# A hybrid decoder layer on one core: the orders of the engines planned by the scheduler's timeline simulation instead of its plain timing

## The chip, the cores and the metric

One core of a Trainium2 chip. TensorE (PE) multiplies matrices, VectorE (DVE), ScalarE (ACT) and GpSimd (POOL) work elementwise, and SyncE (SP) mostly starts DMA transfers; ACT and POOL start some too. The metric is the device time of one execution in microseconds, the median of several runs.

## The reference

One layer on x of 1024 tokens by 1024 channels, all in float32. With rmsnorm(x, g) = x · rsqrt(mean(x²) + eps) · g:

```
h = x
f = swiglu(rmsnorm(h, ffn1_pre_g), ffn1_w_gu, ffn1_w_down)     # 1024 -> 2 x 2816 -> 1024
h = h + 0.5 * rmsnorm(f, ffn1_post_g)
m = hybrid_mixer(rmsnorm(h, mix_pre_g), w_in, ...)              # below
h = h + rmsnorm(m, mix_post_g)
c = memory_cross_attention(rmsnorm(h, xa_pre_g), rmsnorm(mem, mem_g), xa_wq, xa_wkv, xa_wo)
h = h + rmsnorm(c, xa_post_g)
f = swiglu(rmsnorm(h, ffn2_pre_g), ffn2_w_gu, ffn2_w_down)
h = h + 0.5 * rmsnorm(f, ffn2_post_g)
```

The mixer projects its input, runs 16 heads of stick-breaking attention (width 64, blocks of 128) on one half of the projection and a chunked state-space scan (SSD: 16 heads, 2 groups, state 128, chunks of 128, after a short convolution) on the other, normalises both, and multiplies the two by w_out. The cross-attention has 4 heads of 256 over 256 memory tokens.

## The kernel before, in words

Everything is kept transposed, channels on partitions, and the tokens are two halves of 512. Every product of matrices is made of three passes of a reduced-precision float type: an operand is split into a high part, which ScalarE casts (line 263, or line 270 with a scale), and a low part, the difference, which VectorE subtracts (line 265 or 272). TensorE multiplies high by high, low by high and high by low (line 138). So each weight tile and each activation passes through a cast and a subtraction before TensorE can use it. In the names, whi and wlo are the parts of a weight, xh and xl, S, hl, ohi and olo those of an activation; wraw and raw are weights as loaded, mm and dn banks of PSUM with sums, ms the bank of the norms.

The stages follow one another in the profiled execution like this: ffn1 up to about 450 us, ffn1 down to 690, SSD to 1016, attention to 1585, mix_out (the product with w_out) to 1740, cross-attention to 1985, ffn2 up to 2440, ffn2 down to the end. In the ffn stages, after a few plain tiles, sums and differences of operands are formed so that seven products do for eight (a Strassen step): GpSimd adds weights (line 737), ScalarE scales blocks of the input that are loaded again (line 666), VectorE combines them (lines 676 and 679), ScalarE and VectorE split the result; the epilogue adds the seven results (lines 793 to 818).

A norm works like this: squares are made on ScalarE and added on VectorE (`sumsq`, lines 374 to 385), a column product on TensorE sums over channels (`rms_cols`, line 317; in the rows ms<-small,acc), a square root on ScalarE, which needs its table loaded, and a reciprocal on VectorE give the factors, and two row products with a diagonal matrix (`rms_rows`, line 341; ms<-dg and ms<-rpre or ms<-rn) spread them over partitions. Later steps multiply sums in PSUM by these rows and so let the banks free.

What sets the order: the author has fixed TensorE's. `_pe` (line 100) ties each matmul to the one before it by a dependence without a semaphore:

```
if self.prev is not None:
    self._after(ins, self.prev)
self.prev = ins
```

Only groups inside `with self.pinned(at)` (line 144), which are column and row products of norms, are not in this chain: each group has to come before the matmul at which a clock of the author's own passes `at`, and where before that is left to the scheduler. Work put on a list for later is emitted at fixed points of that clock and kept in program order (`kp`, line 117), and a few steps have a raised priority (`urgent`, line 96). All else, the orders on VectorE, ScalarE and GpSimd and that of the loads on SyncE, is chosen by the scheduler, which runs a model of the engines over the whole program and issues at each time what is ready, by priority. The allocation of slots in SBUF and PSUM pools follows from that order. The scheduler is set up in `build`, line 2412.

Of the kernel before, what the change touches and what calls it, by code (L numbers as in the profile page):

```python
# [2402 lines left out]
def build(arrays):  # L2403
    nc = bacc.Bacc("TRN2", target_bir_lowering=False, num_devices=1)
    ap = {
        n: nc.dram_tensor(f"in_{n}", v.shape, mybir.dt.from_np(v.dtype), kind="ExternalInput").ap()
        for n, v in arrays.items()
    }
    ap["out"] = [
        nc.dram_tensor(n, v, F32, kind="ExternalOutput").ap() for n, v in (("out_a", (H, D_MODEL)), ("out_b", (H, D_MODEL)))  # L2410
    ]
    with tile.TileContext(nc) as tc:
        Kern(nc, tc, ap).run()
    return nc

# [7 lines left out]
```

## Time and profile before

| | |
|---|---|
| median of 3 runs | 2643.67 us (2641.38 to 2644.43) |
| profiled execution, and its span | 2645.18 us, 2643.4 us |
| busy: PE, DVE, ACT, POOL | 2576.9, 1983.2, 1262.9, 530.8 us |
| mean granted clock of TensorE | 0.992 |
| moved by DMA | 528.87 MB, 200 GB/s |

A row of the timeline has a start and a length in us, the engine, the line, the operation, out<-in by the program's names, and in brackets how long the engine stood idle before it and who released it. A row of the waits has who waited for whom, and the us in total, the times and the longest. Times count from the span's start. A matmul of 512 columns is 0.39 us long but overlaps the next; they start 0.227 us apart when nothing holds them.

### The profile page before, as it was taken

Reading aid. Unit: us, or ns where it says so; the run is one execution under the profiler, and the core shown is the slowest. Engines: PE = TensorE matmul, PEld = TensorE weight load, DVE = VectorE, ACT = ScalarE, POOL = GpSimd, SP = SyncE. Lnnn points to the kernel's source line nnn. Section 1 sums busy time; section 2 is a strip of 40 time slices with the busy share of each in tenths; the row PEclk is TensorE's granted clock in tenths of the full one; section 3 lists DMA queues with packets and bytes.
Section 4 is the critical chain, followed back from the end, with each engine's and each line's share of the span. In section 5 each row is a group of like instructions: output and inputs, shape, how many; then the busy total and the mean of one; then the engine's idle time right before and its main releaser. Section 6 shows DMA issues by size and latency. Waiting matters only on the chain.

```text
span 2643.4 us, 36454 instructions
## 1 busy us (share of the span) xinstructions
PE 2576.9 (97%) x12598; PEld 2135.0 (81%) x12598; DVE 1983.2 (75%) x3085; ACT 1262.9 (48%) x2276; POOL 530.8 (20%) x660
## 2 busy tenths in 40 slices
PE   8999999999999999999999998999999999999998
PEld 6788888887777778888888787887878788888887
DVE  7888787888678774777777777775448989895675
ACT  7544443545367783445554445254445433333432
POOL 1555552001100000000000001122012555542000
PEclk9999999999999999999999999999999999999999
DMA  5688887754721226433434458777667455555976
GB/s 209 238 308 302 304 282 252 255 193 158 259 79 45 71 70 196 115 99 108 109 108 115 146 178 323 252 274 252 218 230 272 167 187 203 195 180 210 347 276 218
DMA packets 225241, 528.87 MB, mean 200 GB/s; under 512 B 28064, under 2 KB 35104, under 8 KB 225056
## 3 DMA queue, kind: packets, MB, share of 16 engines
q1 hardware_dynamic: 190432, 419.56, 48.2%
q0 software_dynamic: 27424, 93.87, 9.8%
q10 hardware_dynamic: 7200, 13.11, 1.3%
q8 instruction: 99, 1.62, 0.3%
q14 instruction: 86, 0.70, 0.1%
HBM read 353.41 MB, written 152.04 MB: 191 GB/s over the span
## 4 chain that ended last, share of the span: by engine, by line
PE 79%; DVE 9%; DMA 6%; ACT 3%; issue 2%; POOL 1%; SPq 0%; DVEq 0%; ACTq 0%; POOLq 0%
PE mm L138 45%; PE dn L138 24%; PE z L138 2%; PE ms L138 2%; PE tr L141 2%; PE y L138 1%; PE ms L141 1%; DMA wraw<-act 1%; DMA raw<-act 1%; DVE hl L265 1%; DVE wlo L265 1%; PE seg L138 1%; DMA blk<-h 1%; DVE whi L265 0%; DMA oraw<-mix 0%
## 5 line engine op out<-in xcount | busy, mean ns | idle before, releaser
L138 PE MATMUL mm<-xh,whi 128*128 128x512 f32 x1288 | 511.5, 406 | 11.1 <-ACT xh L270 7.0
L138 PE MATMUL mm<-xh,wlo 128*128 128x512 f32 x1240 | 478.5, 393 | 3.2 <-DVE wlo L265 2.9
L138 PE MATMUL mm<-xl,whi 128*128 128x512 f32 x1188 | 467.8, 394 | 1.0 <-DVE xl L265 0.7
L138 PEld LDWEIGHTS mm<-xh,whi 128*128 128x128 f32 x1288 | 244.1, 189 | 53.6 <-ACT xh L270 6.9
L138 PEld LDWEIGHTS mm<-xh,wlo 128*128 128x128 f32 x1240 | 234.3, 189 | 55.3 <-DVE wlo L265 3.4
L138 PEld LDWEIGHTS mm<-xl,whi 128*128 128x128 f32 x1188 | 225.6, 190 | 34.1 <-DVE xl L265 1.8
L1823 DVE TENSOR_TENSOR_SCAN nb<-nb,begin 128x128 f32<-128x128 f32 (+7 forms) x128 | 171.7, 1352 | 55.0 <-ACT nb L1819 54.4
L1819 ACT ACTIVATE nb<-z,scale 128x128 f32<-128x128 f32 (+2 forms) x192 | 107.8, 580 | 88.8 <-PE z L138 87.7
L263 ACT CAST whi<-wraw 128x1024 fp32r<-128x1024 f32 (+1 forms) x89 | 81.2, 914 | 69.1 <-PE mm L138 39.1
L1856 POOL MEMSET ath<- 128x128 f32 x64 | 13.1, 205 | 499.0 <-PE mm L138 499.0
L265 DVE TENSOR_TENSOR wlo<-wraw,whi 128x1024 fp32r<-128x1024 f32 x61 | 74.4, 1220 | 38.3 <-ACT whi L263 38.0
L138 PE MATMUL dn<-xh,wlo 128*128 128x512 f32 x296 | 101.0, 389 | 0.0
L737 POOL TENSOR_TENSOR wc<-wraw,raw 128x512 f32<-128x512 f32 x57 | 87.5, 1535 | 66.6 <-DVE whi L265 30.7
L737 POOL TENSOR_TENSOR wc<-raw,wraw 128x512 f32<-128x512 f32 x55 | 85.5, 1555 | 66.5 <-DVE wlo L265 31.4
L819 POOL TENSOR_TENSOR ft<-ft,e 128x512 f32<-128x512 f32 x38 | 62.4, 1642 | 144.2 <-DVE e L818 85.7
L650 ACT ACTIVATE ft<-ft 128x512 f32<-128x512 f32 x88 | 55.4, 631 | 75.0 <-DVE ft L649 70.3
L263 ACT CAST ath<-tr 128x512 fp32r<-128x512 f32 (+1 forms) x107 | 58.2, 545 | 67.5 <-PE tr L141 66.1
L138 PE MATMUL dn<-xh,blk 128*128 128x512 f32 x280 | 90.2, 389 | 0.0
L265 DVE TENSOR_TENSOR atl<-tr,ath 128x512 fp32r<-128x512 f32 (+1 forms) x107 | 67.0, 629 | 29.2 <-ACT ath L263 28.9
L138 PE MATMUL dn<-xh,whi 128*128 128x512 f32 x256 | 88.0, 389 | 0.0
L138 PE MATMUL mm<-ath,v 128*128 128x256 f32 x320 | 86.2, 291 | 0.6 <-DVE sq L1838 0.6
L382 DVE TENSOR_TENSOR acc<-acc,sq 128x512 f32<-128x512 f32 x78 | 52.3, 684 | 42.5 <-ACT sq L381 42.2
(586 smaller groups left out, 6667.9 us busy)
## 6 DMA issues: line engine op xcount, KB each, us to landing
whi<-dwhi SPq DMA_DIRECT2D x57, 512.0 KB, 3.4
wlo<-dwlo SPq DMA_DIRECT2D x57, 512.0 KB, 4.2
wraw<-act SPq DMA_DIRECT2D x102, 256.0 KB, 4.4
raw<-act SPq DMA_DIRECT2D x96, 256.0 KB, 4.3
wraw<-in_w_gu SPq DMA_DIRECT2D x44, 512.0 KB, 4.4
raw<-in_w_gu SPq DMA_DIRECT2D x38, 512.0 KB, 4.8
khi<-whi POOLq DMA_DIRECT2D x30, 512.0 KB, 4.6
klo<-wlo POOLq DMA_DIRECT2D x30, 512.0 KB, 6.7
```

What stands on the lines that cost most here:

```text
L138: self._pe(self.nc.tensor.matmul(out, lhsT, rhs, start=start, stop=stop, skip_group_check=self.more), cost)
L141: self._pe(self.nc.tensor.transpose(out, src, self.ident if ident is None else ident), 109.0)
L263: self.kp(self.nc.scalar.copy(hi, src))
L265: (eng or self.nc.vector).tensor_tensor(out=lo, in0=src, in1=hi.bitcast(F32), op=ALU.subtract)
L382: self.kp(nc.vector.tensor_tensor(out=accs[i % 2], in0=accs[i % 2], in1=sq, op=ALU.add))
L650: nc.scalar.activation(t, t, AF.Silu)
L737: nc.gpsimd.tensor_tensor(out=t, in0=a, in1=b, op=op)
L819: nc.gpsimd.tensor_tensor(out=t1, in0=t1, in1=e, op=ALU.mult)
L1819: nc.scalar.activation(nb[:, s0:s1], z[:, 0:n], AF.Sigmoid, scale=sc[:, i : i + 1])
L1823: nc.vector.tensor_tensor_scan(out=nb[:, 0:Wd][:, ::-1], data0=nb[:, 0:Wd][:, ::-1], data1=begin[:, S - Wd : S][:, ::-1], initial=0.0, op0 ...
L1856: nc.gpsimd.memset(x[:, 0, :].bitcast(F32), 0.0)
```

## The change

The one changed line tells the scheduler to plan with its timeline simulation, another model of how long instructions take and when they are ready, where it used its plain timing. The program that goes into the scheduler, every operation and every tile, is the same; priorities, the fixed chain on TensorE and the program order of later work still hold.

```
-    with tile.TileContext(nc) as tc:
+    with tile.TileContext(nc, schedule_with_timeline_sim=True) as tc:
```

What comes out differs. On TensorE ten floating norm groups take other places (168 lines of difference on 9885 rows), and nothing else moves. On VectorE 2326 lines differ, on ScalarE 1314, on SyncE 950, on GpSimd 205. ScalarE has 59 table loads where it had 56. 360 tiles get another slot.

At the start of the program, on ScalarE, the splits of the first half of x (xh), the squares of the first norm (acc, sq) and the casts of the first weights (whi) stand like this before:

```order
L263 CAST whi_196<-wraw_194 128x1024
L270 ACTIVATE xh_4_80<-S_68_182,params_78 128x512
L270 ACTIVATE xh_5_81<-S_68_182,params_78 128x512
L270 ACTIVATE xh_6_82<-S_69_183,params_78 128x512
L270 ACTIVATE xh_7_83<-S_69_183,params_78 128x512
L270 ACTIVATE xh_8_84<-S_70_184,params_78 128x512
L270 ACTIVATE xh_9_85<-S_70_184,params_78 128x512
L270 ACTIVATE xh_10_86<-S_71_185,params_78 128x512
L270 ACTIVATE xh_11_87<-S_71_185,params_78 128x512
L378 ACTIVATE acc_87_236<-S_68_182 128x512
L378 ACTIVATE acc_88_237<-S_68_182 128x512
L263 CAST whi_226<-wraw_224 128x1024
```

Now, from the second of those squares to the same cast:

```order
L378 ACTIVATE acc_88_237<-S_68_182 128x512
L270 ACTIVATE xh_6_82<-S_69_183,params_78 128x512
L381 ACTIVATE sq_89_240<-S_69_183 128x512
L270 ACTIVATE xh_7_83<-S_69_183,params_78 128x512
L381 ACTIVATE sq_90_243<-S_69_183 128x512
L270 ACTIVATE xh_8_84<-S_70_184,params_78 128x512
L270 ACTIVATE xh_9_85<-S_70_184,params_78 128x512
L270 ACTIVATE xh_10_86<-S_71_185,params_78 128x512
L381 ACTIVATE sq_91_246<-S_70_184 128x512
L270 ACTIVATE xh_11_87<-S_71_185,params_78 128x512
L381 ACTIVATE sq_92_249<-S_70_184 128x512
L263 CAST whi_226<-wraw_224 128x1024
```

Of the eight squares of that norm, two stood ahead of the cast whi_226, and now six do, between the splits.

In the same stretch, on TensorE, the column products of that norm (ms_260) among the third weight tile's matmuls (mm_418), the second piece of the difference (in the first, the group's old place goes, behind xh_6):

```order
 L138 MATMUL mm_418<-xh_9_85,wlo_282 128x512
 L138 MATMUL mm_418<-xh_10_86,whi_281 128x512
+L138 MATMUL ms_260<-small_114,acc_87_236 128x1 x4
 L138 MATMUL mm_418<-xl_26_102,whi_281 128x512
 L138 MATMUL mm_418<-xh_10_86,wlo_282 128x512
 L138 MATMUL mm_418<-xh_11_87,whi_281 128x512
-L138 MATMUL ms_274<-dg_270,onesr_115 128x512
 L138 MATMUL mm_418<-xl_27_103,whi_281 128x512
 L138 MATMUL mm_418<-xh_11_87,wlo_282 128x512
+L138 MATMUL ms_274<-dg_270,onesr_115 128x512
 L138 MATMUL ms_274<-rpre_99_271,onesr_115 128x512
```

The group went from behind the seventh of the tile's matmuls to behind the nineteenth, twelve matmuls on; its row products (ms_274) went two on, to the end of the tile.

In the first seven-product of ffn1 up, on ScalarE, the scale of the last operand block (blk_945), the casts of operands (xh) and the casts of weight sums (whi, wlo; wc is a sum made by GpSimd) before:

```order
L666 ACTIVATE blk_861<-blk_861,params_78 128x512
L666 ACTIVATE blk_945<-blk_945,params_78 128x512
L263 CAST blk_1010<-wc_1008 128x512
L263 CAST xh_14_90<-bl_952 128x512
L263 CAST blk_1029<-wc_1027 128x512
L263 CAST xh_15_91<-bh_982 128x512
L263 CAST blk_1049<-wraw_875 128x512
L263 CAST whi_1070<-wc_1068 128x512
L263 CAST whi_1113<-raw_277_873 128x512
L263 CAST wlo_1091<-wc_1089 128x512
```

And now:

```order
L666 ACTIVATE blk_861<-blk_861,params_78 128x512
L263 CAST blk_1010<-wc_1008 128x512
L263 CAST xh_14_90<-bl_952 128x512
L263 CAST blk_1029<-wc_1027 128x512
L263 CAST whi_1070<-wc_1068 128x512
L263 CAST whi_1113<-raw_277_873 128x512
L263 CAST wlo_1091<-wc_1089 128x512
L666 ACTIVATE blk_945<-blk_945,params_78 128x512
L263 CAST wlo_1134<-wc_1132 128x512
L263 CAST xh_15_91<-bh_982 128x512
L263 CAST blk_1049<-wraw_875 128x512
```

The scale blk_945 stood right behind that of blk_861 and now stands behind three weight casts, and the cast xh_15 that it leads to stands behind a fourth.

At the end of the SSD, on ScalarE, up to the exponential of one chunk (the L1415 on L_9204; rb are scaled decays for TensorE, zs the gate with its Silu, sq squares of the memory norm) before:

```order
L1409 ACTIVATE rb_9197<-csr_7089,params_78 128x128 x2
L1542 ACTIVATE sq_1971_9169<-wraw_9164 128x256
L1409 ACTIVATE rb_9197<-csr_7089,params_78 128x128
L1542 ACTIVATE sq_1972_9172<-wraw_9164 128x256
L1409 ACTIVATE rb_9265<-csr_7089,params_78 128x128
L1414 ACTIVATE L_9204<-seg_9202 128x512
L1542 ACTIVATE sq_1973_9175<-wraw_9164 128x256
L1415 ACTIVATE L_9204<-L_9204 128x512
```

And now:

```order
L1542 ACTIVATE sq_1973_9175<-wraw_9164 128x256
L263 CAST whi_9188<-wraw_9186 128x1024
L1291 ACT_TABLE_LOAD
L1291 ACTIVATE zs_8970<-zs_8970 128x1024
L1414 ACTIVATE L_9204<-seg_9202 128x512
L1422 ACT_TABLE_LOAD
L1422 ACTIVATE E_9209<-seg_9207 128x512
L1423 ACTIVATE ed_9210<-seg_9207 128x4
L1409 ACTIVATE rb_9328<-csr_7089,params_78 128x128 x4
L1415 ACTIVATE L_9204<-L_9204 128x512
```

The weight cast, the Silu with a table load, four scalings and a second table load came ahead of that exponential.

## The prediction

> **What bounds the kernel now.** I read the page first: the engine totals, then the chain that ended last.
>
> ```profile
> PE 2576.9 (97%) x12598; PEld 2135.0 (81%) x12598; DVE 1983.2 (75%) x3085; ACT 1262.9 (48%) x2276; POOL 530.8 (20%) x660
> PE 79%; DVE 9%; DMA 6%; ACT 3%; issue 2%; POOL 1%; SPq 0%; DVEq 0%; ACTq 0%; POOLq 0%
> ```
>
> TensorE is the bound. Its busy time leaves 2643.4 − 2576.9 = 66.5 us of the span, and its matmuls stand in the same order after the change but for ten small groups, so a new order of the other engines can win no more than these 66.5 us and what the stalls do to the clock. There is no such bound on what it can lose. Next I asked who TensorE waited for (us in total, times, longest), and for windows of 66 us, to see the clock (columns: window, length, busy and count of PE, PEld, DVE, ACT, POOL, then granted clock).
>
> ```profile
> PE mm L138 <- DVE e L798: 5.0, 2, 3.8
> PE dn L138 <- DVE acc L384: 4.7, 1, 4.7
> ```
> ```profile
> 594.00:660.00 66.00, 60.29 (x255) 49.11 (x254) 59.70 (x102) 37.47 (x63) 8.64 (x16) 0.95 0.51 159
> 1782.00:1848.00 66.00, 63.05 (x319) 52.90 (x318) 35.20 (x90) 28.94 (x61) 13.38 (x25) 0.97 0.77 253
> 2046.00:2112.00 66.00, 59.94 (x250) 47.98 (x249) 62.54 (x74) 28.62 (x50) 37.52 (x29) 0.95 0.50 174
> 2112.00:2178.00 66.00, 66.00 (x293) 54.66 (x292) 58.91 (x73) 25.70 (x45) 32.90 (x25) 1.00 0.53 183
> ```
>
> The waits are single events of 1 to 5 us. Where one is long, the clock is below 1: 0.95 of 66 us is 66 × 0.05 = 3.3 us of lost clock, 0.97 about 2 us. Where there is none (last row) TensorE is full and the clock whole. So a new stall of 3 us or more costs its length and, by these rows, 2 to 3.3 us more.
>
> [...]
>
> **The change, part by part.** No operation changes, so each price is a chain: which instruction now stands ahead of one that TensorE waits for, by how much that one comes later, less the slack it had.
>
> *Start (0 to 42 us).* Rows of ScalarE, VectorE, then TensorE:
>
> ```profile
> 12.08 1.14 ACT L378 ACTIVATE acc<-S 128x512 f32<-128x512 f32 x2
> 13.13 1.03 ACT L263 CAST whi<-wraw 128x1024 fp32r<-128x1024 f32 x1
> ```
> ```profile
> 14.19 1.23 DVE L265 TENSOR_TENSOR wlo<-wraw,whi 128x1024 fp32r<-128x1024 f32 x1 [1.23 <-ACT whi L263]
> ```
> ```profile
> 16.04 0.39 PE L138 MATMUL mm<-xh,wlo 128*128 128x512 f32 x1
> ...
> 22.62 0.95 PE L138 MATMUL ms<-small,acc 128*128 128x1 f32 x8
> ...
> 30.19 0.50 PE L138 MATMUL mm<-xh,whi 128*128 128x512 f32 x1 [1.40 <-DVE ft L649]
> ```
>
> Two squares stand ahead of the second weight's cast; now six do. Four more at (13.13 − 12.08)/2 = 0.52 us make 2.1 us. The low half then ends at 15.42 + 2.1 = 17.5 us and not before the matmul at 16.04: slack 0.6, TensorE later by about 1.6. Second, the column matmuls of the first norm stand twelve matmuls later, 12 × 0.227 = 2.7 us (pitch from these rows: 29 matmuls between 16.04 and 22.62 us). The chain from them to the matmul at 30.19, which waits for a bank of PSUM that the norm's factor lets free, is the same 30.19 − 22.62 = 7.57 us, and TensorE stood idle for it already. So 1.6 + 2.7 = **+4.3**, between +2.7 and +5.
>
> *First seven-product of ffn1 (62 to 108 us).* The operands of a product are scaled on ScalarE, combined and split on VectorE and ScalarE. Rows of ScalarE, VectorE, GpSimd, TensorE:
>
> ```profile
> 92.65 0.72 ACT L666 ACTIVATE blk<-blk,params 128x512 f32<-128x512 f32 x1 [1.99 <-DMA blk<-in_xT]
> ...
> 97.50 0.63 ACT L263 CAST whi<-wc 128x512 fp32r<-128x512 f32 x1 [1.53 <-POOL wc L737]
> ```
> ```profile
> 95.64 0.68 DVE L265 TENSOR_TENSOR xl<-bh,xh 128x512 fp32r<-128x512 f32 x1
> ```
> ```profile
> 95.86 1.60 POOL L737 TENSOR_TENSOR wc<-raw,wraw 128x512 f32<-128x512 f32 x1 [3.52 <-ACT xh L263]
> 98.16 1.61 POOL L737 TENSOR_TENSOR wc<-wraw,raw 128x512 f32<-128x512 f32 x1 [0.70 <-ACT whi L263]
> ```
> ```profile
> 96.38 0.51 PE L138 MATMUL mm<-xl,whi 128*128 128x512 f32 x1 [0.24 <-DVE xl L265]
> ```
>
> TensorE already waits for this operand. Its scale (92.65) now stands behind three weight casts, two of which wait for a GpSimd sum of 1.6 us each. Without the wait for the operand ahead of them those sums could start about 1.8 us earlier than in the rows, at 94.1; they end near 98.0, the scale runs at 98.6, its combination and cast follow a third sum's cast that stands ahead too, and the last split ends at 102.8 where it ended at 96.3: **+6.4**, of which I take back 1.4 us at TensorE's next wait (117 us), which the delay covers: +5, between 0 (if GpSimd were ahead) and +7.3 (if its sums start no earlier than in the rows). A stall of this size takes the clock down too: +3.3.
>
> *End of ffn1 down (600 to 690 us).* Rows of VectorE and TensorE:
>
> ```profile
> 612.74 0.68 DVE L265 TENSOR_TENSOR hl<-raw,hl 128x512 fp32r<-128x512 f32 x1
> 613.34 0.68 DVE L384 TENSOR_TENSOR acc<-acc,acc 128x512 f32<-128x512 f32 x1
> ```
> ```profile
> 614.07 1.87 PE L138 MATMUL dn<-small,acc 128*128 128x1 f32 x8 [4.70 <-DVE acc L384]
> ```
>
> The last addition of the squares' sums moves from VectorE's row 719 to 726: seven instructions at 0.605 us, +4.2 us on a stall that is there already, less 1.07 us at the next one (622.7): +3.2. The second norm's sum, at 668 us, comes 1.4 us later, its factor rows 0.9 us earlier. **+3.7**, from 3 to 5, and the longer half-clock stretch +1.7.
>
> *End of the SSD (955 to 1016 us).* Rows of ScalarE, then TensorE:
>
> ```profile
> 975.19 0.62 ACT L1415 ACTIVATE L<-L 128x512 f32<-128x512 f32 x1
> ...
> 980.29 1.28 ACT L1291 ACT_TABLE_LOAD   x1
> 981.59 1.06 ACT L1291 ACTIVATE zs<-zs 128x1024 f32<-128x1024 f32 x1
> ```
> ```profile
> 982.47 0.60 PE L138 MATMUL st<-xdec,Bl 128*128 128x256 f32 x2
> ...
> 994.95 0.63 PE L138 MATMUL ms<-dg,onesr 128*128 128x256 f32 x2
> ```
>
> The gate's Silu with its table load (1.28 + 1.06), a weight cast (1.03), four scalings and a second table load now stand ahead of the exponential at 975.19: about +8 us. The state matmul of that chunk (982.47) had some 5.5 us of slack: +2.5. The memory norm's factor, once behind one table load, now is behind a Silu and two: +3.2 at 994.95. One stall of 1.3 us at 973.8 goes, since its scalings come earlier. **+4.4**, from 3 to 6, and +1.7 of clock.
>
> In the orders ScalarE has 59 table loads where it had 56. [...]
>
> *mix_out, xattn.* TensorE rows:
>
> ```profile
> 1603.15 0.94 PE L138 MATMUL ms<-small,asum 128*128 128x1 f32 x7 [1.40 <-DVE asum L2009]
> ...
> 1612.72 0.47 PE L138 MATMUL ms<-dg,onesr 128*128 128x512 f32 x1 [2.26 <-DVE dg L358]
> ...
> 1790.64 0.50 PE L138 MATMUL mm<-xh,wlo 128*128 128x512 f32 x1 [2.95 <-DVE wlo L265]
> ```
>
> The attention norm's column matmuls move some 45 matmuls down, its row matmuls to five matmuls behind them. The first wait (1.4) goes, but the chain between the two, 1612.72 − 1604.09 = 8.6 us in the rows with other work in between, is no longer covered: shortest 2.3 us (its own instructions), less five matmuls of 0.23, and then 2.2 us until the first result is scaled. **+1**, from −4 to +6. In xattn the weight load that makes the wait at 1790.64 is issued some 4 us earlier and that wait with its clock loss should go (−2.9 − 1.7), but VectorE puts the last norm's updates ahead of a softmax split that TensorE takes at 1771 us: +3.9 and +0.9. **0**, from −4.6 to +3.
>
> *ffn2 up (2040 to 2065 us).* VectorE, TensorE:
>
> ```profile
> 2040.83 0.68 DVE L265 TENSOR_TENSOR S<-wc,S 128x512 fp32r<-128x512 f32 x1
> ```
> ```profile
> 2052.69 0.50 PE L138 MATMUL mm<-xl,wlo 128*128 128x512 f32 x1 [0.71 <-DVE xl L265]
> ```
>
> Seven splits and epilogue steps that stood between the operand combinations from 2040.83 on now stand ahead of them, and the last of the seven waits for ScalarE until 2049. TensorE waits for that chain at 2052.69 and 2061.99. If the chain ran from 2049 without pauses, its sixteen steps of 0.63 us would end at 2059 where they ended at 2057.5, and the splits that TensorE takes on the way come 2 to 7.6 us late: **+5** between these, clock +1.7.
>
> *The rest.* In the middle of ffn1 down VectorE's sums go earlier and the splits later; the slack of the splits falls from 6 to 12 us to 1 to 3 us by the rows, but stays above nothing: 0. SSD start, attention and its end, ffn2 entry and ffn2 down each have chains late by 1 to 3 us against slack that I have not resolved: **+2** together, from −5 to +8.
>
> **Sum.** 4.3 + 5 + 3.7 + 4.4 + 1 + 0 + 5 + 2 = 25.4 us of stalls, and clock 3.3 + 1.7 + 1.7 + 1.7 = 8.4: about +34. Later stalls take up part of what earlier delays do (a late stream finds its operands ready); I take off 4 of it for the places that I saw only one by one. +30 on the profiled execution (2643.4 of span and 1.8 around it, 2645.2) is 2675; the median of the runs is 1.5 us lower: **2673.7 us**.
>
> **The rivals.**
>
> *The losses are covered, the gains are real: faster.* VectorE is idle 25% and ScalarE 52%; if in the changed run both get ahead of TensorE at the start and before 96 and 2052 us, those terms vanish, and what remains are the waits that the new order removes: 2.95 and 1.7 of clock at 1790.64, 1.40 and 2.26 at mix_out with 2 of clock, 1.3 at 973.8: −11.6, so 2632. It decides at the split at 95.64: if that comes no later than 96.3, this holds. For it: the order moves loads ahead that were last. Against: the chains at 30.19 and 96.38 had no slack at all, and their predecessors were moved behind instructions with known durations. Chance 0.13, all faster.
>
> *Everything is hidden: no change.* The moved instructions fall into idle time, gains and losses of 5 us cancel: 2644. For it: ten groups only move on TensorE. Against: the same. Chance 0.08. (0.2% is 5.3 us, about what a measurement of this kernel can tell from no change.)
>
> *The thin cover of ffn1 down breaks.* The sums' stores and loads go around by DMA before the splits can be made; VectorE waited 2.85 us for one of these loads at 601 us. If the six groups of loads each come 3 us later than the slack, TensorE waits 6 × 3 = 18 us more, with its clock 6 × 1.7: 2673.7 + 28 = 2702. For it: slack of 1 to 3 us. Against: the DMA engines are busy by half there (0.51 in the row of 594 us). Chance 0.17, all slower.
>
> The forecast itself has 0.62, of which 0.03 lies within 0.2% of no change and 0.01 below it. Together faster 0.14, same 0.11, slower 0.75. The range for 8 in 10: the forecast's terms at their low ends sum to −3, at their high ends, with clock, to +56, and neither end comes all at once; it reaches down into the two other cases no further than 2645 and up past the broken cover: **2645 to 2710**.
>
> **What would show it.** Right: TensorE's busy time as before but the span longer; the norm's bank wait near 30 us grown from 1.4 to 4 us or more; a wait on the split xl near 100 us of 4 to 7 us with a clock below 1 in 66 to 132 us (now whole); the wait on acc L384 grown from 4.7 to 8; new waits on xdec and on dg near 985 and 998 us; no 2.95 at mm <- wlo near 1790. Wrong: the clock whole in 66 to 132 us, or the total of TensorE's waits below today's; then the steps that order ScalarE and VectorE by the rows' durations fail. A loss in attention or in ffn2 down would be one that I have not priced.

## The result, and the profile after

The kernel after took 2703.24 us (median of 4 runs, 2700.9 to 2709.97) beside 2644.05 for the kernel before (2641.38 to 2646.38, 4 runs): a ratio of 1.0228, 95% interval 1.0208 to 1.0249. It is slower, as forecast, and the time lies in the range; but the forecast was +30 us and the loss is 59. The profiled execution of after took 2700.9 us, its span is 2699.1, 55.7 us more than before's.

The page's engine totals after:

```profile
PE 2596.9 (96%) x12598; PEld 2146.1 (80%) x12598; DVE 1974.5 (73%) x3085; ACT 1269.2 (47%) x2279; POOL 535.9 (20%) x660
```

The 55.7 us have two parts. TensorE's idle time went from 66.5 to 2699.1 − 2596.9 = 102.2, +35.7. Its busy time went from 2576.9 to 2596.9, +20.0, with the same matmuls: that part is the clock, whose mean fell from 0.992 to 0.983. Who TensorE waited for after, of 32 rows those that the argument needs (us in total, times, longest):

```profile
PE mm L138 <- ACT xh L263: 13.0, 3, 5.4
PE ms L138 <- DVE dg L358: 10.6, 4, 5.2
PE dn L138 <- DVE acc L384: 6.3, 1, 6.3
PE seg L138 <- ACT Bl L1401: 5.4, 6, 2.4
PE mm L138 <- DVE e L798: 1.9, 1, 1.9
```

The 2.95 us for wlo are gone. Of the 3.8 us for e, 1.86 are left at the same place, where the same steps of VectorE stand ahead of e in both traces. The wait for acc grew from 4.7 to 6.3; the casts xh, the norm's factors dg, and the decays Bl have new or longer ones. Two of the windows shown of before and two more, after (the third number from the end is the clock):

```profile
66.00:132.00 66.00, 56.31 (x232) 44.80 (x231) 52.90 (x67) 31.31 (x54) 33.20 (x33) 0.92 0.60 204
594.00:660.00 66.00, 59.70 (x252) 49.11 (x252) 54.67 (x94) 32.92 (x58) 3.24 (x6) 0.92 0.48 154
990.00:1056.00 66.00, 56.36 (x383) 49.40 (x383) 40.89 (x84) 38.62 (x66) 3.69 (x4) 0.92 0.39 130
2046.00:2112.00 66.00, 57.18 (x236) 45.47 (x236) 51.60 (x78) 36.91 (x61) 21.55 (x34) 0.90 0.69 243
```

The two that the prediction does not show, before:

```profile
66.00:132.00 66.00, 63.33 (x274) 50.78 (x273) 58.90 (x75) 35.08 (x62) 39.32 (x36) 1.00 0.69 238
990.00:1056.00 66.00, 65.89 (x431) 58.37 (x430) 33.18 (x67) 25.06 (x42) 5.36 (x11) 1.00 0.60 189
```

In these four windows the clock fell by 0.03 to 0.08; in 1650 to 1716 us it fell from 1.00 to 0.92, and in the two others that the prediction shows it is 0.97 each, where it was 0.97 and 1.00. To see where the time came in, I listed TensorE's idle stretches of 1.6 us and more from the timelines of both traces, by place, and paired the matmuls of the two traces to see how much later each place leaves TensorE than it found it ("delay"; it holds idle time and clock):

```
place                    before: us (count)   after: us (count)   delay   forecast, clock in
start, 0-62                  6.95 (1)             8.79 (2)         +4.7     +4.3
first seven-product          0    (0)             7.43 (2)        +10.0     +8.3
ffn1 down                    7.24 (2)             9.63 (2)         -1.1     +5.4
SSD end and behind it        0    (0)             8.78 (3)        +13.2     +6.1
mix_out                      3.95 (2)             5.18 (1)         +0.4     +1
cross-attention, start       2.95 (1)             3.87 (2)         +1.8      0
ffn2 up                      3.83 (1)             9.74 (3)         +7.3     +6.7
the rest                     9.05 (4)            17.24 (8)        +19.4     +2
later stalls take up                                               none     -4
sum                         33.97 (11)           70.66 (23)       +55.7    +30
```

So at the seven named places the forecast is 31.8 and the traces show 36.3; the miss is in the rest (17 us), at the SSD end (7) and in the 4 us taken off, less what ffn1 down gave back. A single pair of profiles leaves 1 to 2 us open at each place, and at ffn1 down, as the control shows below, more. And there are 12 more stalls of this length; 20.0 us of lost clock are 1.67 for each of them in the mean, but single ones cost between nothing and 3.7 us (see the last section).

One correction of the text ahead of the prediction: it says that a group inside `pinned(at)` has to come before the matmul at which the clock passes `at`. The dependence that `_pe` adds is the other way round: the group comes after that matmul, and how long after is what the scheduler chooses. No step of the sum rests on it.

### The profile page after: what moved, and what is told of

Its sections match the earlier page's. It is cut to its first block, busy times and chain, and to the rows that moved or that the text cites. A ratio compares the mean times of both kernels' runs of the same rounds, so it can differ in the third digit from the quotient of the medians.

```text
span 2699.1 us, 36454 instructions
## 1 busy us (share of the span) xinstructions
PE 2596.9 (96%) x12598; PEld 2146.1 (80%) x12598; DVE 1974.5 (73%) x3085; ACT 1269.2 (47%) x2279; POOL 535.9 (20%) x660
## 4 chain that ended last, share of the span: by engine, by line
PE 77%; DVE 9%; DMA 6%; ACT 5%; issue 3%; POOL 0%; SPq 0%; DVEq 0%; ACTq 0%
PE mm L138 44%; PE dn L138 24%; PE z L138 2%; PE ms L138 2%; PE tr L141 2%; DMA wraw<-act 1%; DMA raw<-act 1%; DMA raw<-in_w_dn 1%; PE ms L141 1%; PE y L138 1%; DVE wlo L265 1%; DVE hl L265 1%; DVE whi L265 1%; PE seg L138 1%; DVE xl L272 0%
## 5 line engine op out<-in xcount | busy, mean ns | idle before, releaser
L138 PEld LDWEIGHTS mm<-xl,whi 128*128 128x128 f32 x1188 | 226.6, 191 | 35.7 <-DVE xl L265 3.0
L265 DVE TENSOR_TENSOR wlo<-wraw,whi 128x1024 fp32r<-128x1024 f32 x61 | 74.4, 1221 | 41.3 <-ACT whi L263 41.1
L265 DVE TENSOR_TENSOR atl<-tr,ath 128x512 fp32r<-128x512 f32 (+1 forms) x107 | 67.2, 630 | 32.4 <-ACT ath L263 32.2
L138 PE MATMUL mm<-atl,v 128*128 128x256 f32 x320 | 83.1, 281 | 1.1 <-DVE atl L265 1.1
```

What stands on the lines that cost most here:

```text
L138: self._pe(self.nc.tensor.matmul(out, lhsT, rhs, start=start, stop=stop, skip_group_check=self.more), cost)
L265: (eng or self.nc.vector).tensor_tensor(out=lo, in0=src, in1=hi.bitcast(F32), op=ALU.subtract)
```

## The experiments

Eighteen kernels. All keep every operation and are made in one way: the planner is handed, for each engine, the order that it has to keep, as dependences without semaphores (TensorE's floating groups are held between two neighbours); a few orders have single instructions moved by hand:

```diff
+def hold(nc, tc):
+    ins = {i.name: i for i in nc.cur_bb.bb.instructions}
+    for order in ORDERS:
+        row = [ins[f"I-{n}"] for n in order if f"I-{n}" in ins]
+        for a, b in zip(row, row[1:]):
+            tc.add_manual_dep(b, a.name, NOSYNC, reason="order")
```

So a stretch of one kernel's order can be put into the other's, and the edits below say which. Each ran beside the kernel before on its chip (2638.0 to 2643.0 there), so the ratios compare best; after's is 1.0228, and 0.1% is 2.6 us.

**The named places, or the rest?** The seven places that the prediction priced lie in six stretches of before, 619 us together.

```diff
-ORDERS = after's
+ORDERS = after's, before's at the seven named places     # named_undone
+ORDERS = before's, after's at the seven named places     # rest_undone
```

> The changed kernel, with the order of before put back on all engines in the six stretches that the prediction priced (0 to 135, 600 to 692, 945 to 1052, 1575 to 1640, 1730 to 1800, 1970 to 2120 us of before). Theory A, the terms were about right and the rest of the program, put at +2, was mis-sized: TensorE's starts in the two traces lie 36.6 us further apart over these stretches and 19 us over the others, so this run keeps the 19: 2663. Rival B, the rest costs little by itself and was only late because of what was handed down from the priced stretches: 2646 or less.

> The complement: the order of before everywhere but in the six priced stretches, which keep the new order. Theory A: 2644 + 36.6 = 2681, and the losses in the two complements add up to the whole 59. Rival B: 2700 or more, since the priced stretches carry all of it. If the two sum to clearly more or less than 59, the places are not independent.

Measured: 2661.19, ratio 1.0070 (1.0055 to 1.0085), and 2681.99, ratio 1.0153 (1.0136 to 1.0170). The rest costs 0.70%, 18 us, the named places 1.53%, 40 us; together 2.23% of the 2.28%. The losses add up within some 8 us, the three intervals taken together, so the 4 us that later stalls were to take up are neither shown nor excluded. The rest was the largest error of the sum.

**The rest in three.**

```diff
-ORDERS = after's
+ORDERS = after's, before's in 692-945                                  # rest_ssd
+ORDERS = after's, before's in 1052-1575                                # rest_attn
+ORDERS = after's, before's in 135-600, 1640-1730, 1800-1970, 2120-end  # rest_tail
```

> The kernel after the change with before's order of all engines in 692 to 945 us, the SSD stage up to its end. Nothing is left out. The prediction's sum gave the whole rest of the kernel outside its named places +2 us, and the run with before's order at the named places showed about 19.7. Theory (the rest's loss is many waits of a few us, sitting where the delay of the two profiles grows): 4 to 9 us less than after, 2694 to 2699, as the delay grows by 4.4 us near 770 and by 3.0 near 870. Rival (the rest's loss has no place of its own, and is the clock): within 2 us of after.

> The kernel after the change with before's order of all engines in 1052 to 1575 us, the k/v projections and the self-attention. Nothing is left out. Theory (as the delay of the two profiles grows there by 4.9 us and falls by 0.8 at the end): 3 to 6 us less than after, 2697 to 2700. Rival (no place of its own): within 2 us of after.

> The kernel after the change with before's order of all engines in 135 to 600, 1640 to 1730, 1800 to 1970 and from 2120 us to the end: ffn1's middle, the entry and the rest of the cross-attention, and ffn2's down product. Nothing is left out. Theory (the delay of the two profiles grows by 4.3 us in the cross-attention's rest and by 2.8 in ffn2 down): 6 to 9 us less than after, 2694 to 2697; with the two other runs of this batch the three add up to some 20 us. Rival (no place of its own): within 2 us of after.

Measured: 2692.62, ratio 1.0203 (1.0189 to 1.0217); 2699.23, 1.0231 (1.0217 to 1.0245); 2692.13, 1.0207 (1.0193 to 1.0221). By the ratios, 6.6 us come back in the SSD, none in attention, 5.5 in the tail: 11 of the 18, with about 4 us of uncertainty on each. In the SSD the waits are seen to shrink: those of 2.43 and 2.28 us are 0.81 and 1.70 in rest_ssd, as in before, and that of 1.89 is gone; a wait of 1.64 that before has at 839.51 is back. TensorE's rows there after, then the first in rest_ssd:

```profile
780.55 0.49 PE L138 MATMUL seg<-Ct,Bt 128*128 128x128 f32 x2 [2.43 <-ACT Bl L1401]
794.21 0.91 PE L138 MATMUL st<-xdec,Bl 128*128 128x256 f32 x2 [2.28 <-DVE xdec L1444]
916.06 0.50 PE L138 MATMUL seg<-rb,csc 128*128 128x512 f32 x1 [1.89 <-ACT Bl L1401]
```
```profile
777.87 0.49 PE L138 MATMUL seg<-Ct,Bt 128*128 128x128 f32 x2 [0.81 <-ACT Bl L1401]
```

So the theory holds for the SSD, by time and trace, and for the tail by time, a little under what was expected; for attention the time shows nothing, and some 7 us of the rest stay without a place in the times. The trace of rest_attn has a part of them: three waits of 1.97 us for v (1207.88, 1330.90 and 1393.19 after) are 0.80 there, 3.5 us less, of which 2.4 are lost again at mix_out in that profile.

**The first seven-product: which cause?** The prediction blamed one chain on ScalarE. u_chain takes that chain back alone, u_act_dve all of VectorE and ScalarE there, u_pool_sp all of SyncE and GpSimd:

```diff
 ORDERS = after's
+ACT: blk_945's scale back behind blk_861's, the cast xh_15 back ahead of blk_1049; DVE: its bh and xl back   # u_chain
+before's in 60-135 on ACT and DVE                                                                         # u_act_dve
+before's in 60-135 on SP and POOL                                                                         # u_pool_sp
```

> The changed kernel, with four instructions of the first seven-product moved back: the scale of the last operand block and the cast of its operand on ScalarE, its combination and its low half on VectorE. The prediction's step (that chain behind the weight casts costs +5 to +6.4, and its stall the clock): the waits for ScalarE's cast near 108 us go, 2703 - 6 to 8 = 2695 to 2697. Rival (the loss of 10 us there comes from VectorE's other moves, which make the second and third operands late before): 2 us or less, 2701 to 2703.

> The changed kernel, with the order of before on ScalarE and VectorE in the first seven-product (60 to 135 us), the new one on SyncE and GpSimd. Theory: the 10 us lost there are the orders of these two engines (of VectorE's most of all, since the one chain moved back gave next to nothing): 2703 - 10 = 2693. Rival: GpSimd's order, which sets when its sums hold VectorE up, costs them: 2701 to 2703.

> The complement in the same stretch: the order of before on SyncE and GpSimd, the new one on ScalarE and VectorE. Theory: 2702 to 2704. Rival: 2693.

Measured: 2701.48, ratio 1.0229 (1.0214 to 1.0244); 2691.14, 1.0191 (1.0175 to 1.0206); 2704.08, 1.0234 (1.0219 to 1.0249). ScalarE around the scale after, TensorE after and in u_chain, and the window in u_act_dve:

```profile
104.86 0.62 ACT L263 CAST wlo<-wc 128x512 fp32r<-128x512 f32 x1 [1.73 <-POOL wc L737]
105.38 0.72 ACT L666 ACTIVATE blk<-blk,params 128x512 f32<-128x512 f32 x1
...
107.74 0.62 ACT L263 CAST xh<-bh 128x512 fp32r<-128x512 f32 x1 [0.59 <-DVE bh L679]
```
```profile
108.41 0.79 PE L138 MATMUL mm<-xh,whi 128*128 128x512 f32 x1 [5.12 <-ACT xh L263]
```
```profile
106.01 0.79 PE L138 MATMUL mm<-xh,whi 128*128 128x512 f32 x1 [3.15 <-ACT xh L263]
108.27 0.79 PE L138 MATMUL mm<-xl,whi 128*128 128x512 f32 x1 [1.47 <-DVE xl L265]
```
```profile
66.00:132.00 66.00, 61.64 (x266) 49.35 (x265) 57.51 (x75) 33.87 (x58) 35.02 (x35) 1.00 0.64 214
```

The chain of the prediction is there as written: the scale waits behind a cast that waits for GpSimd's sum, the cast xh comes at 107.74, and TensorE has waited 5.12 us. But with the chain taken back TensorE still waits 3.15 and 1.47. The kept traces show why. ScalarE's scale in u_chain, then the load of the last block on GpSimd's queue, before and in u_chain:

```profile
104.21 0.72 ACT L666 ACTIVATE blk<-blk,params 128x512 f32<-128x512 f32 x1 [5.54 <-DMA blk<-in_xT]
```
```profile
85.77 1.06 POOL L663 DMA_DIRECT2D blk<-in_xT  x2 [0.17 <-issue]
```
```profile
95.62 1.09 POOL L663 DMA_DIRECT2D blk<-in_xT  x2 [0.85 <-DVE bl L679]
```

The scale no longer stands behind casts, but the block that it scales has only just landed: 104.21 where after has 105.38. GpSimd starts that load 9.9 us later than before (9.3 in after, at 95.03), behind VectorE's combination bl. So two chains led to the same operand, about 1 us apart: the chain at the scale ended last, and it was not the cause alone. No run takes VectorE's order back by itself. With both engines' orders taken back the load starts at 93.37 and the scale at 99.79, the clock is whole again, TensorE is busy 61.64 us of the window instead of 56.31, and 10 to 12 us come back.

**The end of the SSD: one engine or two?**

```diff
 ORDERS = after's
+ACT: Silu zs_8970 behind the next weight cast, Silu zs_9192 behind cmem         # ssd_silu
+ACT: Silu zs_8970 behind the next exponential L_9272, zs_9192 behind cmem;
+DVE: zs_8970's product (L1516) behind the next xdec, zs_9192's behind dg        # ssd_both
+before's in 1003-1052, all engines                                              # kv_tail
```

> The changed kernel, with two instructions of ScalarE moved back at the end of the SSD: the gate's Silu behind the exponential that it stood ahead of, the next gate's Silu behind the memory norm's square root. The prediction's step: waits of 2 to 2.5 us on xdec and of 3.2 us on dg go, with their clock: 2703 - 6 to 9 = 2694 to 2697, if table load and Silu are what delays both chains. Rival (the weight cast, the scalings and VectorE's order hold them up anyway): 2 us or less, 2701 or more.

> The kernel after the change with two moves at the end of the SSD loop, on ScalarE and VectorE both: the gate's Silu at L1291 goes behind the work of the head that is due (the first behind the second head's exponentials, into the 5.6 us in which ScalarE waits for a matmul, the second behind the memory norm's factor), and VectorE's product at L1516, which needs the Silu, goes behind xdec and behind dg. Nothing is left out. Theory (the prediction's steps at the SSD end, with the addition that VectorE's order held the same decision): the waits of 2.28 and 2.02 us for xdec and of 3.16 us for dg all but go, 5 to 7 us of stall and up to 2 us of slow clock behind them: 2694 to 2698. Rival (the stalls only move to the next head or to the k/v tail behind it, as with ScalarE's move alone): within 2.5 us of that run, 2698 to 2702.

> The changed kernel, with the order of before on all engines in the keys and values of the memory (1003 to 1052 us of before), where a wait of 3.6 us on VectorE's sq of line 1560 stands in the trace after that the prediction had not priced. Theory: the new order there (VectorE's additions of squares ahead of the freeing of a bank) makes it: 2703 - 5 = 2698. Rival: it was handed down from the norm's late factor at 1023 us: 2702 to 2704.

Measured: 2700.48, ratio 1.0224 (1.0208 to 1.0239); 2699.99, 1.0218 (1.0202 to 1.0234); 2701.85, 1.0230 (1.0210 to 1.0250). TensorE after, VectorE and TensorE in ssd_silu, TensorE in ssd_both:

```profile
1005.99 1.06 PE L138 MATMUL st<-xdec,Bl 128*128 128x256 f32 x2 [2.02 <-DVE xdec L1444]
1023.17 0.82 PE L138 MATMUL ms<-dg,onesr 128*128 128x256 f32 x2 [3.16 <-DVE dg L358]
1046.84 0.36 PE L138 MATMUL mm<-xs,whi 128*128 128x256 f32 x1 [3.60 <-DVE sq L1560]
1655.20 0.77 PE L138 MATMUL ms<-dg,onesr 128*128 128x512 f32 x1 [5.18 <-DVE dg L358]
```
```profile
1003.11 0.69 DVE L1516 TENSOR_TENSOR zs<-zs,xs 128x512 f32<-128x512 f32 x1 [2.69 <-ACT zs L1291]
```
```profile
1004.79 1.22 PE L138 MATMUL st<-xdec,Bl 128*128 128x256 f32 x2 [3.14 <-DVE xdec L1444]
```
```profile
1016.01 0.63 PE L138 MATMUL ms<-dg,onesr 128*128 128x256 f32 x2 [1.02 <-DVE dg L358]
1040.62 0.56 PE L138 MATMUL mm<-xs,whi 128*128 128x256 f32 x1 [5.27 <-DVE sq L1560]
1656.17 0.77 PE L138 MATMUL ms<-dg,onesr 128*128 128x512 f32 x1 [7.63 <-DVE dg L358]
```

With only ScalarE's Silu moved, the waits stay (3.14 us for xdec, 3.28 for dg), since VectorE's product, which needs the Silu, stands ahead of xdec: VectorE now waits 2.69 us for it. The order holds the same decision twice. With both moved the wait for xdec is gone, that for dg is 1.02, and TensorE is 7.2 us earlier at the memory norm, 8 us behind it, as the theory said. But the time shows 0.1%, less than can be told from nothing. In that profile the wait of the k/v tail is 1.7 us longer (3.60 becomes 5.27). In attention two waits of 1.97 us (1202.70 and 1389.47) take the clock down to 0.83 over 10 us, 1.7 us each, where after has the same two waits at a clock of 1.00. And mix_out's factor waits 7.63 us instead of 5.18; that wait is between 4.68 and 7.75 in the kernels with the new order there, so it isn't shown that the gain made it longer. The mechanism of the waits is shown, a gain in time is not. Taking back the tail's order alone cut its wait to 1.22 and the time by nothing that can be told.

**ffn1 down.**

```diff
+ORDERS = before's, after's in 600-692     # d_only
+ORDERS = after's, before's in 600-692     # d_undone
+ORDERS = before's                         # held_before
```

> The kernel before, with the new order of all engines in the end of ffn1 down alone (600 to 692 us). The prediction's step: seven instructions more ahead of the addition of the squares, +3.7 of waiting and +1.7 of clock, 2649.4; nothing hides it when nothing earlier is late. Rival, from the trace after, where this stretch gained 1.1 us: the additions find VectorE idle, which waited for loads there, and the time is 2643, within 0.1% of before.

> The kernel after the change with before's order of all engines in 600 to 692 us, the ffn1 down product's end. Nothing is left out. Theory (the prediction's step D, and the timed run with the new order there alone, which was 4.7 us slower): 4 to 6 us less than after, 2697 to 2700. Rival (the profiles, whose delay of the matmuls behind this stretch is about 1 us less than ahead of it): no less than after, 2702 to 2705.

> The control: the kernel before's own order of every engine, given to the planner as a list that it has to keep, as all the kernels with a part of one order and a part of the other are made. Nothing is left out. Theory (what these kernels show is the order): the time of before, within 0.1%, 2639 to 2645. Rival (the way in which an order is held costs time itself, so that the 4.7 us of the ffn1 down product's order alone and the 3 to 8 us of the cross-attention's order alone are not the order's): 3 to 8 us more than before.

Measured: 2646.15, ratio 1.0019 (1.0010 to 1.0029); 2700.36, 1.0222 (1.0205 to 1.0240); the control 2644.40, 1.0008 (0.9996 to 1.0020). TensorE after:

```profile
630.22 1.87 PE L138 MATMUL dn<-small,acc 128*128 128x1 f32 x8 [6.30 <-DVE acc L384]
684.22 1.05 PE L138 MATMUL ms<-small,acc 128*128 128x1 f32 x8 [3.33 <-DVE acc L384]
```

Less the control, the new order there costs 3 us; taken back, it gives 1.6: both within their intervals of nothing. The two waits are 9.63 us where before they and the two for the factors behind them were 4.70 + 0.91 + 2.54 + 0.57 = 8.72. The prediction's 5.4 was too much. Why the first wait grew by 1.6 and not by 4.2 can be read from VectorE's last step that waits for a load ahead of the sum, before and after:

```profile
606.12 0.69 DVE L976 TENSOR_TENSOR wraw<-wraw 128x512 f32<-128x512 f32 x1 [1.18 <-DMA wraw<-act]
```
```profile
618.04 0.69 DVE L976 TENSOR_TENSOR wraw<-wraw 128x512 f32<-128x512 f32 x1 [0.58 <-DMA wraw<-act]
```

From there to the sum (613.34 before, 629.48 after) it is 7.22 us before and 11.44 after: the 4.2 us of the seven instructions are there. But TensorE, 14.6 us late by then, comes 2.6 us later against that load than before, and waits so much less. How much it waits hangs on the load: the control has before's order, its load came 3.0 us earlier (603.12), and it waits 1.14 us for the sum and 2.22 for the factor. Against the control, d_only's 5.34 us for the sum is the forecast 4.2 more; but the wait for the factor is gone there.

**The cross-attention's start.**

```diff
+ORDERS = before's, after's in 1730-1800 on SP and POOL     # x1_loads
+ORDERS = before's, after's in 1730-1800 on all engines     # x1_all
```

> The kernel before with the new order of the DMA queues (SyncE and GpSimd) in 1730 to 1800 us alone. Nothing is left out. Theory (the prediction's gain at 1790.64, where TensorE waited 2.95 us for a load of wlo that stood fourth in the queue and now stands third): 2.9 us of stall and up to 1.7 us of slow clock go, 2637 to 2639 beside 2641.5 to 2644. Rival (the load is bound by the transfer and not by its place in the queue, or the next load is late in its place): as before, within 1 us.

> The kernel before with the new order of all engines in 1730 to 1800 us, the start of the cross-attention, where the new order of the DMA queues alone cost 14 us because a load of v stood behind stores of tiles that VectorE's old order made later. Nothing is left out. Theory (the prediction's X1: a gain of 2.9 us of wait and 1.7 of clock at 1790.64 against a loss of 3.9 and 0.9 at 1771): within 3 us of before, 2640 to 2646, and no wait for v. Rival (the queue order is the loss by itself): 2652 to 2658, with a wait of over 5 us for v.

Measured: 2657.11, ratio 1.0055 (1.0041 to 1.0069), a loss where both theories expected a gain or nothing; and 2646.14, 1.0025 (1.0015 to 1.0035), a loss of 6.6 us where the theory allowed 3. These rows are of best_hand (below), which has the same queues there: TensorE, then GpSimd's queue, and that queue's row in before:

```profile
1801.82 2.90 PE L138 MATMUL dn<-pt,v 128*128 128x512 f32 x6 [11.74 <-DMA v<-kv]
```
```profile
1789.83 0.54 POOL L194 DMA_DIRECT2D klo<-wlo  x1 [6.68 <-DVE st L2129]
1790.35 1.08 POOL L437 DMA_DIRECT2D h<-F  x2
1791.42 0.56 POOL L2093 DMA_DIRECT2D v<-kv  x1
```
```profile
1776.94 0.54 POOL L2093 DMA_DIRECT2D v<-kv  x1 [1.41 <-PE dn L138]
```

The load of v was issued 14 us later than before, because in the new queue it stands behind a store of klo and stores of h, which wait for VectorE, and VectorE still had its old order. With all engines in the new order there is no wait for v, the 2.95 us for wlo are gone, and two waits of 1.89 and 1.95 us for pt are there; less the control, 0.17% stays, at the edge of what can be told. A queue's order belongs to the orders that feed it: with the queues alone the wait for wlo at 1790.64 stays as well (2.95 us in best_hand), so the gain that the prediction hoped for was not to be had from them.

**Orders by hand.** From before's own order: e (a sum of a seven-product's epilogue, which the expectations call the delta rule's) ahead of the split that it stood behind, the sums acc ahead of weights at two places, mix_out's floating groups later, and x1_loads; then without the sums and without x1_loads.

```diff
 ORDERS = before's
+DVE: e_20203 (L798) ahead of blk_20319; PE: ms_15762 8, ms_15776 16 and 15 matmuls later     # both
+DVE: acc (L384) ahead of dx_5852 and hl_5869, and ahead of wlo_6438; SP, POOL: x1_loads       # best_hand
```

> The kernel before with its own order held but for a few moves by hand at its longest stalls: on VectorE the delta rule's e at L798 ahead of the weight's low half at L265 that it stood behind (the 3.83-us wait at 2086.33), the sum acc at L384 ahead of a weight's low half (L265) at two places of the ffn1 down product (the stalls at 614 and 668), the new queue order at 1730 to 1800 us, and on TensorE the norm's four sum matmuls 8 matmuls later and the two matmuls of its factor 16 and 15 matmuls later in mix_out (the stalls at 1613 and 1623). Nothing is left out. Theory (what bounds the kernel is a handful of waits that an order of the engines' queues decides, each of which costs its length and a stretch of slow clock behind it): 12 to 18 us less than before, 2626 to 2632. Rival (the clock and the stalls behind take the gain back, as the kernel as a whole is bound by TensorE's own 2600 us): less than 6 us, 2638 or more.

> The kernel before's own order held but for two places at which the trace showed a gain that stayed: on VectorE the delta rule's e at L798 ahead of the weight's low half that it stood behind (the 3.83-us wait at 2086.33), and on TensorE in mix_out the norm's four sum matmuls 8 matmuls later and the two matmuls of its factor 16 and 15 matmuls later. Nothing is left out. Theory (the curve of the earlier run by hand, where 2 us stayed won behind mix_out and 1.6 us behind the delta rule): 3 to 4 us less than the control. Rival (the next wait takes all of it): the control's time within 2 us.

Measured: 2659.35, ratio 1.0065 (1.0051 to 1.0079), so about 0.1% above x1_loads, which it contains; and 2642.14, 1.0005 (0.9994 to 1.0016), the control's time. The 12 to 18 us did not come. For two_places its rival holds, a next wait that takes all of it; x1_loads, which best_hand contains, has nearly all of best_hand's loss. In ffn1 down of best_hand, TensorE and VectorE:

```profile
609.24 1.05 PE L138 MATMUL dn<-small,acc 128*128 128x1 f32 x8 [0.41 <-DVE acc L384]
619.08 0.79 PE L138 MATMUL dn<-dg,onesr 128*128 128x512 f32 x1 [4.99 <-DVE dg L358]
```
```profile
609.10 0.69 DVE L265 TENSOR_TENSOR dx<-xl,dx 128x512 fp32r<-128x512 f32 x1
...
616.93 0.15 DVE L332 TENSOR_TENSOR cpost<-dn,cpre 128x4 f32<-128x4 f32 x1
```

The 4.70 us for the sum are 0.41, and the 0.91 us for its factor dg are 4.99: the column sum is there at 609.24 + 1.05 = 610.3, but the factor's first step (L332) stands in VectorE's order behind the splits from 609.10 on and comes at 616.93. Here moving one step handed the idle time to the next. No version here beats the kernel before.

## Why the prediction was right or wrong

- *Direction: right.* "There is no such bound on what it can lose" and the chains priced one by one gave slower at 0.75. Of the signs, the waits on xdec and dg and the end of the 2.95 us came; "TensorE's busy time as before" did not, and it went badly with the sum's own 8.4 us of clock.
- *A number met by luck:* the rival "The thin cover of ffn1 down breaks" gives 2702 for the measured 2703.24, but that stretch cost 0 to 3 us.
- *Start: the number right, in part by luck.* +4.3 forecast, all of it stall, +4.7 in the traces: the waits there grew by 1.9 us (now 1.74, 0.34 and 1.40 near 30 us, and 0.54 at 16.97), and a clock of 0.95 in 0 to 66 us, 3.3 us, which the step left out, made up the rest.
- *Small slips, 0.1 or 0.2 us each:* 2.1 less a slack of 0.6 is 1.5 and not 1.6; the wait at 622.7 is 0.91 in before and not 1.07; the one at 973.8 is 1.18 and not 1.3.
- *First seven-product: size near, cause half right.* 8.3 forecast, 10.0 in the traces, 10 to 12 by u_act_dve. The chain at the scale blk_945 is in the trace, but the block's load, 9 us late behind VectorE, would have held the same operand 1 us less; the prediction did not price it.
- *ffn1 down: too much,* 5.4 for what the runs put between 0 and 3. The seven instructions cost their 4.2 us on VectorE; how much of that TensorE waits hangs on when the load comes and when TensorE arrives, which the step took from one profile.
- *End of the SSD: mis-sized,* 6.1 for 13.2. The waits for xdec and dg came (2.02, 3.16), though VectorE's product holds them as much as ScalarE's Silu; a wait of 3.60 us for sq at 1046.84 was not seen, and a clock of 0.92 behind them costs 5.3 where 1.7 stood.
- *mix_out, cross-attention's start, ffn2 up: right within 2 us,* by the traces; only the cross-attention's start has a run of its own. In mix_out it came through another wait than before (5.18 for dg), the first wait gone; at the cross-attention's start as forecast, the 2.95 us gone and 1.92 and 1.95 new for pt (3.9 was forecast).
- *The step that failed:* the term for the rest. "SSD start, attention and its end, ffn2 entry and ffn2 down each have chains late by 1 to 3 us against slack that I have not resolved: +2 together." named_undone measured 18 us for it, clock included. A plan that differs in thousands of rows has losses at places that one doesn't look at, and here they did not cancel.
- *"Later stalls take up part of what earlier delays do … I take off 4":* not shown. The halves add up to the whole within 8 us. Single places do take up delay, as ffn1 down's wait took 2.6 us.
- *Clock: 8.4 forecast, 20.0 measured.* "a new stall of 3 us or more costs its length and, by these rows, 2 to 3.3 us more" left out the shorter stalls. A row of before shows one, and could have been read:

```profile
776.40 0.70 PE L138 MATMUL st<-xdec,Bl 128*128 128x256 f32 x2 [1.70 <-DVE xdec L1444]
...
779.31 0.63 PE L138 MATMUL mm<-xh,whi 128*128 128x512 f32 x1
```
```profile
775.00:785.00 10.00, 8.60 (x47) 6.34 (x47) 5.48 (x13) 8.04 (x16) 0.00 (x0) 0.83 0.00 0
```

Behind a stall of 1.70 us the matmuls last 0.63 instead of 0.39 us for some 3 us (the clock granted from 778 to 780 us is 0.50), and the clock of the 10 us is 0.83: 1.7 us lost. The sum has the same 1.7 behind each of three stalls, where the prediction names no row for it. The 12 additional stalls of 1.6 us and more, at 1.7 each, are 20.4; the busy time grew by 20.0. That is a mean and in part luck: not every such stall lowers the clock, and the long ones cost up to 3.7 us (behind the 6.30 at 630.22, a clock of 0.63 over 10 us). Part of this clock belongs to the rest.

Why the timeline simulation's plan is worse than the plain timing's, the runs do not tell: they tell where its orders lose.

## What to carry to other kernels

When a planner is exchanged, price lost clock for stalls from 1.6 us on and not from 3 (here 20.0 us were lost, with 12 more stalls of that length), ask for each moved chain whether a second engine's order holds the same decision and whether a load on the same operand is late too, and don't price the stretches not looked at near zero: here they lost 18 us, beside 40 at the places that looked worst. A single chain that ended last was not the only late one: taking it back gave at most 2 of 12 us. The order of one queue or one engine, taken alone, lost 14 us or won nothing: it fits the orders of the engines that feed it.

## What the runs showed of the hardware that I had not expected

Stalls well under 3 us lowered the clock at some places and not at others. After has the same as before's row at 776.40 (1.70 us, a clock of 0.83 over 10 us): the 1.89 us at 916.06, shown above, and

```profile
915.00:925.00 10.00, 8.94 (x48) 6.83 (x50) 6.38 (x16) 5.51 (x17) 0.00 (x0) 0.83 0.01 2
```

The control has the stall of before's row at 776.40 once more, with the same length, and loses nothing (a clock of 1.00); nor does after behind the 1.97 us at 1207.88. TensorE and window in the control, then the window after:

```profile
774.56 0.70 PE L138 MATMUL st<-xdec,Bl 128*128 128x256 f32 x2 [1.70 <-DVE xdec L1444]
```
```profile
775.00:785.00 10.00, 10.00 (x62) 7.81 (x61) 6.33 (x16) 8.60 (x18) 0.00 (x0) 1.00 0.00 0
```
```profile
1205.00:1215.00 10.00, 8.03 (x56) 7.12 (x54) 8.10 (x16) 4.43 (x9) 0.34 (x2) 1.00 0.62 173
```

So no length between 1.6 and 2.6 us decided it here. I counted in 18 of the 20 traces kept, all but those of x1_loads and two_places: of the stalls with no other of 0.85 us or more within 9 us, a clock below 1 in the next 8 us followed 6 of 61 between 1.0 and 1.6 us, 5 of 17 between 1.6 and 1.8, 28 of 60 between 1.8 and 2.0, 25 of 30 between 2.2 and 2.6 and 62 of 63 between 3.0 and 6.3; many of them are the same place in several kernels.

Many of VectorE's subtractions and combinations lasted longer beside GpSimd's sums, up to three times as long in the rows below (2.08 us beside 0.68). In after none of the 598 subtractions of 128x512 at L265 with no such sum beside them takes over 0.70 us; of the 103 that begin during one, 63 take over 1 us. VectorE and GpSimd after:

```profile
90.35 2.08 DVE L265 TENSOR_TENSOR wlo<-wc,wlo 128x512 fp32r<-128x512 f32 x1
92.36 0.68 DVE L265 TENSOR_TENSOR xl<-bh,xh 128x512 fp32r<-128x512 f32 x1
92.96 1.78 DVE L679 SCALAR_TENSOR_TENSOR bl<-blk,params 128x512 f32<-128x512 f32 x1
```
```profile
90.60 1.27 POOL L737 TENSOR_TENSOR wc<-wraw,raw 128x512 f32<-128x512 f32 x1
92.52 1.67 POOL L737 TENSOR_TENSOR wc<-raw 128x512 f32<-128x512 f32 x1 [0.64 <-DVE wlo L265]
```

The two long ones end 0.6 us behind the sums; the one between them, which began ahead of the second sum, lasts 0.68, and that sum takes 1.67 us instead of 1.27. The prediction's chains took 0.605 or 0.63 us for a step. The long subtraction took 1.4 us more than the one at 92.36, the long combination 1.0 us more than the one at 96.05 (0.75 us).
